# Turning the normed FFN rows in the cross-attention stage, with their combinations stored turned

## The chip, the cores and the metric

One NeuronCore of a Trainium2 chip runs the whole kernel. Its engines are TensorE (PE, with its weight loads listed apart as PEld), VectorE (DVE), ScalarE (ACT), GpSimd (POOL) and the queue engine SyncE (SP), which issues most DMAs; POOL issues the others. Matrix products come out in PSUM, 16 KB in each of 128 partitions; everything else is in SBUF or, between stages, in DRAM. The metric is the device time of one execution in microseconds, the median of several runs.

## What is computed

One layer of a streaming encoder for 2048 prompt rows and 128 sample rows of width 1024: a mixer (banded attention beside a convolution), a cross attention into 256 memory rows, and a SwiGLU FFN, each with a norm ahead of it and one behind. The part that matters here:

```python
h = rmsnorm(x, g_mem_pre)
x = x + rmsnorm(memory_attention(h, mk, mv, w_mq, w_mo), g_mem_post)
h = rmsnorm(x, g_ffn_pre)
f = (jax.nn.silu(h @ w_gate) * (h @ w_up)) @ w_down      # 1024 -> 2816 -> 1024
x = x + rmsnorm(f, g_ffn_post)
```

All in float32. The kernel makes each product from three: both operands are split into a rounded high part and a low part, and hi*hi, hi*lo and lo*hi are summed in PSUM (`mm3`, lines 286 to 290, or `mm3h`, lines 292 to 297).

## The kernel before, in words

**Order of the work.** A tile scheduler sets the order on each engine: it takes the instructions in program order as priority, simulates the engines' times, and adds the semaphores that the data need. Each engine then runs its list in order. Buffers are fixed places in SBUF and PSUM: a `Region` gives each tag a list of places, and one request after the other takes the next place in the list (`at`, `tile`). Two tags may share a place; a later user then waits until the earlier one, in program order, is through.

**Cross attention** (`phase_cross`). Sixteen prompt tiles of 128 rows. The pass of the loop for tile t holds, in program order: `probs` of t (8 transposes of the probabilities into PSUM "t", then a cast on ACT, L1317, and a subtract on DVE, L1318), `scores` of t+1 (48 matmuls of 512 columns, L296, into "s"), `norm` of t+2 (a normed tile, 8 transposes into "t"), `values` of t (48 matmuls into "y", then `postnorm`, L341 to L347: square on ACT (L313), rstd on POOL, scale on DVE (L345), residual add on POOL (L346), store of the tile to `x2` in DRAM). "t" is one buffer at 8 KB of PSUM, "s" one at 12 KB, "y" two at 4 and 0 KB. For tiles 14 and 15 the order is a little different: `probs` of 15 stands in the midst of the values of 14.

**`natural`** (L1331 to L1354). The FFN goes over three groups of rows, `GROUPS`, of up to 384 columns each. It multiplies with fewer products by combining halves, so it wants, for each pair of row tiles (`PAIRS`, three for each group, the last of group 2 being the two halves of the sample tile, 64 rows each), seven combinations of the halves of the two normed tiles, 512 columns wide. `natural` loads the two tiles of a pair into `na` and `nb`, norms them (square L1342, rstd on POOL L1344 and L1345, scale on DVE L1346), makes combinations with four POOL adds (L1347, 1349, 1351, 1353) in `na`, `nb` and `nt`, and stores them with four POOL DMAs to `hn` in DRAM. `na`, `nb` and `nt` are single, at SBUF 0 to 12 KB. The square writes the single scratch buffer `junk`, as the square of `postnorm` does. One pair is done at the end of a pass of the loop as soon as its tiles are there: after t = 4, 5, 6 (group 0), 7 (the sample pair), 10, 11, 12 (group 1) and 15 (pair (2,0)). Pair (2,1) is left for gate-up.

**Gate-up** (`gate_up`). For each group g and each of 22 blocks f of 128 hidden columns: 7 products of 12 matmuls each (`product`, L288 to L290) between a weight combination (`wforms`, made on POOL from two 512 KB loads and split by L1446 on ACT and L1447 on DVE) and a row combination `ts[j]`. The row combinations of a group are made by `tform` (L1415 to L1428): for each of seven, three loads of 256 KB from `hn` (buffer "nat": three of 2 KB), 4 transposes each into PSUM "tr" (L1424), a cast on ACT (L1426) and a subtract on DVE from PSUM (L1427). For group 0 this stands at the start, with raised priority; for groups 1 and 2 between the products of the last block of the group before (`turn`), each combination right behind the product that used its place last: these are the two turns. The products write PSUM places of 2 KB in the order 8, 10, 0, 2, 4, 6 KB.

Of the kernel before, what the change touches and what calls it, by code (L numbers as in the profile page):

```python
# [8 lines left out]
F32 = mybir.dt.float32  # L9
# [3 lines left out]
ALU = mybir.AluOpType  # L13
# [4 lines left out]
P = 128  # L18
D = 1024
KC = D // P  # L20
# [31 lines left out]
TFORM = (0, 5, 1, 2, 4, 6, 3)  # L52
# [34 lines left out]
class Region:  # L87
# [13 lines left out]
    def at(self, tag, kb, *places):  # L101
        self.tags[tag] = [[arena.find(int(o * 256)) for arena, offs in places for o in offs], int(kb * 256), 0]
        return self
# [35 lines left out]
class Build:  # L139
# [82 lines left out]
    def setup(self):  # L222
        nc, A = self.nc, self.A
        enter = lambda n, **kw: self.ctx.enter_context(self.tc.tile_pool(name=self.nm(n), bufs=1, **kw))
        self.const = enter("const")
        self.dpool = enter("dram", space=DRAM)
        sb, ps = enter("sb"), enter("ps", space=PSUM)
        self.sbF = Arena(sb.tile([P, 13120], F32, tag="f", name="sbf"))
        sbr = Arena(sb.tile([P, 22528], F32R, tag="r", name="sbr"))
        self.xctx = ExitStack()  # L230
        sx = self.xctx.enter_context(self.tc.tile_pool(name=self.nm("sx"), bufs=1))
        self.sbR = Joined(sbr, Arena(sx.tile([P, 5120], F32R, tag="x", name="sbx")))
        self.ps = Arena(ps.tile([P, 4096], F32, tag="p", name="psb"))
        self.ident = self.t(self.const, [P, P], F32, "ident")
        make_identity(nc, self.ident)
        self.mhalf = self.t(self.const, [P, 4], F32, "mhalf")
        nc.gpsimd.memset(self.mhalf[:, :], -0.5)
        self.f1s = self.dram("f1s", [P, KC, MH, NM])
        self.f2s = self.dram("f2s", [P, KC, D])
        self.qs = [self.dram(f"qs{i}", [P, 2, NPT * P]) for i in range(4)]  # L240
        self.ks = [self.dram(f"ks{i}", [2, P, NPT * P]) for i in range(4)]
        self.vs = [self.dram(f"vs{i}", [P, 4, NPT, P]) for i in range(2)]
        self.cs = [self.dram(f"cs{i}", [P, 4 * P]) for i in range(NPT + 1)]
        self.x1 = [self.dram(f"x1_{i}", [P, D]) for i in range(NPT + 1)]
        self.x2 = [self.dram(f"x2_{i}", [P, D]) for i in range(NPT + 1)]
        self.hn = [self.dram(f"hn{g}", [P, 3, 7, 512]) for g in range(3)]
        self.af = [self.dram(f"af{g}", [P, NF // 2, 7, 3 * P]) for g in range(3)]
        self.vsamp = self.dram("vsampd", [P, 512])

# [1007 lines left out]
    def phase_cross(self, ctx):  # L1257
        nc, A = self.nc, self.A
        sbF, sbR = self.sbF, self.sbR
# [68 lines left out]

        gffn = self.gain(Region().at("gffn", 4, (self.gffn, [0])), "g_ffn_pre", "gffn")

        def natural(g, p):  # L1331
            n = PAIRS[g][p][2]
            xa = self.t(pool, [P, 2, 512], F32, "na")[:n]
            xb = self.t(pool, [P, 2, 512], F32, "nb")[:n]
            tt = self.t(pool, [P, 2, 512], F32, "nt")[:n]
            dst = self.hn[g]
            for x, (t, r0) in zip((xa, xb), PAIRS[g][p][:2]):
                x2 = x.rearrange("p a b -> p (a b)")
                nc.sync.dma_start(x2, self.x2[t][r0:r0 + n, :])
                junk = self.t(pool, [P, D], BF16, "junk", 1)  # L1340
                ss = self.t(pool, [P, 1], F32, "ss", 6)
                nc.scalar.activation(junk[:n, :], x2, AF.Square, accum_out=ss[:n, :])  # L1342
                r = self.t(pool, [P, 1], F32, "rstd", 6)
                nc.gpsimd.tensor_scalar(r[:n, :], ss[:n, :], 1.0 / D, EPS, ALU.mult, ALU.add)  # L1344
                nc.gpsimd.tensor_tensor(r[:n, :], r[:n, :], self.mhalf[:n, 0:1], ALU.pow)  # L1345
                nc.vector.scalar_tensor_tensor(x2, x2, r[:n, :], gffn[:n, :], ALU.mult, ALU.mult)  # L1346
            nc.gpsimd.tensor_tensor(tt[:, 0, :], xb[:, 0, :], xa[:, 0, :], ALU.subtract)  # L1347
            nc.gpsimd.dma_start(dst[:n, p, 0:2, :], xa)
            nc.gpsimd.tensor_tensor(tt[:, 1, :], xb[:, 1, :], tt[:, 0, :], ALU.subtract)
            nc.gpsimd.dma_start(dst[:n, p, 4:6, :], tt)  # L1350
            nc.gpsimd.tensor_tensor(xb[:, 0, :], xb[:, 1, :], xb[:, 0, :], ALU.subtract)
            nc.gpsimd.dma_start(dst[:n, p, 2:4, :], xb)
            nc.gpsimd.tensor_tensor(xa[:, 1, :], tt[:, 1, :], xa[:, 1, :], ALU.subtract)
            nc.gpsimd.dma_start(dst[:n, p, 6, :], xa[:, 1, :])  # L1354

        self.natural = natural
        todo = [(g, p) for g in range(3) for p in range(3)]
        hq = {0: norm(0)}
        f1 = [load(self.f1s[:, k, :, :].rearrange("p h n -> p (h n)"), f"f1{k}",
# [11 lines left out]
        for t in range(NPT):  # L1371
            pp = probs(z) if t < NPT - 1 else self.last_probs
            if t == 0:
                more(KC, self.last_split)
            if t + 1 < NPT:
                z = scores(*hq[t + 1][1:])
            if t + 2 < NPT:
                hq[t + 2] = norm(t + 2)
            values(t, hq.pop(t)[0], *pp)
            for g, p in list(todo):  # L1380
                ready = all(x == S_TILE or x < t for x, _ in PAIRS[g][p][:2])
                if ready and t >= 4:
                    natural(g, p)
                    todo.remove((g, p))
                    break
        self.todo = todo
# [9 lines left out]
    def gate_up(self, ctx):  # L1396


        nc, A = self.nc, self.A
        sbF, sbR = self.sbF, self.sbR  # L1400
        t6h, t6l, w8, fx, af0, af1 = self.flex(ctx, (1536, F32R), (1536, F32R), (1024, F32R), (1536, F32), (2688, F32),
                                               (2688, F32))
        pool = (Region().at("wf", 4, (sbF, [12, 18, 46.5, 22]))
                .at("s", 2, (sbF, [26, 28, 38.5])).at("nat", 2, (sbF, [40.5, 42.5, 44.5]))
                .at("x1", 1.5, (sbF, [30, 31.5])).at("x2", 1.5, (sbF, [33, 34.5]))
                .at("x3", 1.5, (sbF, [36]), (fx, [0])).at("th", 1.5, (fx, [1.5, 3, 4.5]))
                .at("wh", 2, (sbR, [68, 72, 76, 80, 84, 88, 92, 104]), (w8, [0]))
# [7 lines left out]
        def tform(g, j):  # L1415
            hi = self.t(pool, [P, 4, 3 * P], F32R, f"t{j}h")
            lo = self.t(pool, [P, 4, 3 * P], F32R, f"t{j}l")
            for p in range(3):
                n = PAIRS[g][p][2]
                x = self.t(pool, [P, 512], F32, "nat")  # L1420
                nc.sync.dma_start(x[:n, :], self.hn[g][:n, p, TFORM[j], :])
                ps = self.t(ps_tr, [P, 4, P], F32, "tr")
                for k in range(4):
                    nc.tensor.transpose(ps[:, k, :n], x[:n, k * P:(k + 1) * P], self.ident[:n, :n])  # L1424
                c = slice(p * P, p * P + n)
                nc.scalar.copy(hi[:, :, c], ps[:, :, :n])  # L1426
                nc.vector.tensor_tensor(lo[:, :, c], ps[:, :, :n], hi[:, :, c].bitcast(F32), ALU.subtract)  # L1427
            return hi, lo  # L1428

        def wforms(f):  # L1430
# [30 lines left out]
        for g in range(3):  # L1461
            n = sum(p[2] for p in PAIRS[g])
            for fp in range(NF // 2):
# [4 lines left out]
                for x in range(2):  # L1468
# [45 lines left out]
                    if f < NF - 1 or g < 2:  # L1514
                        w = wforms((f + 1) % NF)
                    if g == 0 and x == 1 and self.todo:
                        self.natural(*self.todo.pop(0))
                self.act_forms(af, g)
                nc.sync.dma_start(self.af[g][:, fp, :, :], af[:, :, :])

# [208 lines left out]
```

## Time and profile before

| what | value |
|---|---|
| median of 3 runs | 3008.1 us (3006.9 to 3008.7) |
| span of the profiled execution | 3000.1 us; the page gives no time of that execution apart from its span |
| PE busy | 2949.2 us |
| cross attention, first to last square of a finished tile (L313) | 1232.5 to 1577.0 us |
| gate-up, first matmul of 384 columns to the end of its stage | 1576.8 to about 2517 us |
| transposes in `tform` (L1424) | 252, at 1564.0 to 2284.1 us |
| turns to group 1 and group 2 | near 1885 to 1960 and 2225 to 2300 us |

The profile is one execution, on one core. Rows of the timeline give start and length in us, engine, line, operation, output and input by the program's names, the number of instructions merged, and in brackets the idle time of the engine ahead of them with what ended it. Matmuls are pipelined: a row's length is longer than the step from one matmul to the next. A row of the windows view gives a stretch and the time that each engine was busy in it; PEclk is the granted TensorE clock as a share of full speed.

### The profile page before, as it was taken

How to read it: one execution, taken by the hardware profiler on the slowest of the kernel's cores; microseconds unless marked ns; L12 is line 12 of the kernel's file. 1: busy time of each engine (PE TensorE's matmuls, PEld its weight loads, DVE VectorE, ACT ScalarE, POOL GpSimd, SP SyncE). 2: the span in 40 equal slices, each digit the busy share in tenths (PEclk: the TensorE clock that was granted, in tenths of full speed). 3: DMA queues.
4: the chain of work that ended last, by engine and by line, in shares of the span. 5: the costliest groups of instructions: out<-in, count | busy, mean ns of one | idle time of the engine just before them, and what ended most of it. 6: DMA issues, size and time to landing. Idle time of an engine off the chain costs nothing.

```text
span 3000.1 us, 46145 instructions
## 1 busy us (share of the span) xinstructions
PE 2949.2 (98%) x16940; PEld 2714.6 (90%) x16940; DVE 2134.6 (71%) x3090; ACT 1360.3 (45%) x2731; POOL 1416.7 (47%) x1338
## 2 busy tenths in 40 slices
PE   9999999999999999999999999999999999999998
PEld 9999999989997887887888999999999999888777
DVE  6687886968776466435358888888788998555666
ACT  5535455668883344323334333433344444433433
POOL 0267496721123244136357565446555775424413
PEclk9999999989999999999999999999999999999999
DMA  7645253664435456323246333544334336756664
GB/s 278 246 138 185 88 170 108 201 213 168 155 138 175 169 199 205 105 87 133 88 163 222 116 137 124 196 153 152 134 134 157 142 140 205 256 176 215 217 223 148
DMA packets 197552, 499.57 MB, mean 167 GB/s; under 512 B 19334, under 2 KB 84750, under 8 KB 188485
## 3 DMA queue, kind: packets, MB, share of 16 engines
q1 hardware_dynamic: 182397, 427.01, 41.9%
q0 software_dynamic: 14928, 69.61, 6.2%
q8 instruction: 133, 2.18, 0.3%
q14 instruction: 94, 0.77, 0.1%
HBM read 365.45 MB, written 141.81 MB: 169 GB/s over the span
## 4 chain that ended last, share of the span: by engine, by line
PE 38%; DMA 4%; issue 3%; DVE 3%; POOL 3%; ACT 0%; SPq 0%; DVEq 0%; POOLq 0%; ACTq 0%
PE psb L290 12%; PE psb L288 12%; PE psb L289 12%; DMA sbf<-in_w_down_dram 2%; POOL sbf L1569 1%; PE psb L296 1%; DMA sbf<-x 1%; PE psb L1424 1%; DMA sbf<-hn 0%; DVE sbr L1639 0%; DVE sbr L1447 0%; POOL sbf L346 0%; DVE sbr L1573 0%; DMA sbf<-in_w_gate_dram 0%; DVE sbx L1447 0%
## 5 line engine op out<-in xcount | busy, mean ns | idle before, releaser
L288 PE MATMUL psb<-sbr 128*128 128x384 f32 (+3 forms) x2808 | 941.7, 337 | 4.1 <-DVE sbx L676 1.6
L289 PE MATMUL psb<-sbr 128*128 128x384 f32 (+3 forms) x2356 | 804.6, 342 | 0.4 <-DVE sbr L338 0.3
L290 PE MATMUL psb<-sbr 128*128 128x512 f32 (+3 forms) x1848 | 633.1, 344 | 4.3 <-DVE sbr L1639 4.1
L288 PEld LDWEIGHTS psb<-sbr 128*128 128x128 f32 x2808 | 529.2, 189 | 34.6 <-ACT sbr L1638 2.8
L290 PE MATMUL psb<-sbr,sbx 128*128 128x384 f32 (+2 forms) x1484 | 475.8, 321 | 0.0
L289 PEld LDWEIGHTS psb<-sbr 128*128 128x128 f32 x2356 | 443.9, 188 | 27.1 <-DVE sbr L1427 0.7
L290 PEld LDWEIGHTS psb<-sbr 128*128 128x128 f32 x1848 | 347.9, 188 | 34.9 <-DVE sbr L1639 8.2
L296 PE MATMUL psb<-sbr 128*128 128x512 f32 x1200 | 295.3, 394 | 1.9 <-ACT sbr L1317 1.1
L1447 DVE TENSOR_TENSOR sbr<-sbf,sbr 128x512 fp32r<-128x512 f32 x258 | 262.7, 1021 | 38.8 <-ACT sbr L1446 37.9
L1446 ACT CAST sbr<-sbf 128x512 fp32r<-128x512 f32 x258 | 159.2, 620 | 277.4 <-PE psb L289 229.3
L290 PEld LDWEIGHTS psb<-sbr,sbx 128*128 128x128 f32 x1484 | 279.6, 189 | 0.2
L542 DVE SCALAR_TENSOR_TENSOR psb<-sbf,psb 128x768 f32<-128x768 f32 (+1 forms) x290 | 264.3, 911 | 6.1
L296 PEld LDWEIGHTS psb<-sbr 128*128 128x128 f32 x1200 | 222.2, 189 | 47.6 <-ACT sbr L1317 1.3
L1639 DVE TENSOR_TENSOR sbr<-sbf,sbr 128x384 fp32r<-128x384 f32 (+2 forms) x242 | 168.1, 717 | 99.2 <-ACT sbr L1638 98.0
L283 POOL TENSOR_TENSOR sbx<-sbf,sbr 128x1024 fp32r<-128x1024 f32 (+1 forms) x62 | 155.0, 2501 | 84.8 <-ACT sbr L281 81.0
L1638 ACT CAST sbr<-sbf 128x384 fp32r<-128x384 f32 (+2 forms) x242 | 112.4, 483 | 174.1 <-PE psb L289 149.8
L1569 POOL TENSOR_TENSOR sbf<-sbf 128x512 f32<-128x512 f32 x77 | 106.5, 1390 | 168.7 <-DMA sbf<-in_w_down_dram 167.1
L552 POOL TENSOR_TENSOR flexb<-flexb,flexb 128x128 f32<-128x128 f32 (+1 forms) x180 | 168.9, 939 | 25.4 <-ACT flexb L551 15.1
L288 PE MATMUL psb<-sbr,sbx 128*128 128x384 f32 (+1 forms) x524 | 170.6, 327 | 1.8 <-ACT sbx L1446 1.1
L1446 ACT CAST sbx<-sbf 128x512 fp32r<-128x512 f32 x153 | 94.7, 620 | 163.4 <-PE psb L289 143.4
L1447 DVE TENSOR_TENSOR sbx<-sbf,sbx 128x512 fp32r<-128x512 f32 x153 | 153.4, 1004 | 17.0 <-ACT sbx L1446 16.8
L1441 POOL TENSOR_TENSOR sbf<-sbf 128x512 f32<-128x512 f32 x66 | 97.5, 1477 | 107.2 <-DVE sbr L1447 50.7
(350 smaller groups left out, 6281.5 us busy)
## 6 DMA issues: line engine op xcount, KB each, us to landing
af<-flexb SPq DMA_DIRECT2D x33, 1344.0 KB, 5.8
sbf<-in_w_down_dram SPq DMA_DIRECT2D x154, 256.0 KB, 3.5
sbf<-in_w_gate_dram SPq DMA_DIRECT2D x66, 512.0 KB, 3.3
sbf<-in_w_up_dram SPq DMA_DIRECT2D x66, 512.0 KB, 3.5
sbf<-af SPq DMA_DIRECT2D x85, 384.0 KB, 4.3
sbf<-x SPq DMA_DIRECT2D x49, 512.0 KB, 3.8
sbf<-in_w_in_dram SPq DMA_DIRECT2D x48, 512.0 KB, 3.8
sbr<-ks POOLq DMA_DIRECT2D x16, 1024.0 KB, 8.6
```

What stands on the lines that cost most here:

```text
L283: self.lo_engine.tensor_tensor(lo[:, c], wf[:, c], hi[:, c].bitcast(F32), ALU.subtract)
L288: nc.tensor.matmul(ps, lh, rh, start=start, stop=False, **kw)
L289: nc.tensor.matmul(ps, lh, rl, start=False, stop=False, **kw)
L290: nc.tensor.matmul(ps, ll, rh, start=False, stop=stop, **kw)
L296: nc.tensor.matmul(y[o], l, r[:, o * 512:(o + 1) * 512], start=start and x == 0, stop=stop and x == 2)
L542: nc.vector.scalar_tensor_tensor(acc if w < CW - 1 else o, src(w), cwt[:, j, w:w + 1], acc, ALU.mult, ALU.add)
L552: nc.gpsimd.tensor_tensor(o, o, v, ALU.add)
L1446: nc.scalar.copy(hs[j][:, :], src[j])
L1447: nc.vector.tensor_tensor(ls[j][:, :], src[j], hs[j][:, :].bitcast(F32), ALU.subtract)
L1569: nc.gpsimd.tensor_tensor(acc[:, :], acc[:, :], q[:, :], ALU.add if s > 0 else ALU.subtract)
L1638: nc.scalar.copy(ch[:, m], a[:, x, m])
L1639: nc.vector.tensor_tensor(cl[:, m], a[:, x, m], ch[:, m].bitcast(F32), ALU.subtract)
```

## The change

`natural` becomes `forms`. It still loads and norms the two tiles of a pair, and then turns each of them: 8 transposes into a PSUM buffer that the caller names ("t" in the cross attention, one buffer for all 8; "tr" in gate-up, two of 4), and two copies on ACT back into the tile's own place, so that `na` and `nb` hold their normed rows turned. The four POOL adds work on the turned tiles as before on the unturned ones, and the four stores write `hn`, which is laid out as 128 partitions by 7 combinations by the three pairs' columns.

`tform` loads a combination of the whole group with one DMA of up to 768 KB, and splits it straight from SBUF: one cast and one subtract for 1536 columns (for group 2 two of each, since its last pair is narrower). Its transposes are gone. "nat" is three buffers of 6 KB in place of three of 2 KB: the first where the three were, at 40.5 KB, the others at 0 and 6 KB of SBUF, on the places of `na`, `nb` and `nt`.

```diff
--- before.py
+++ after.py
@@ -243,7 +243,7 @@
         self.cs = [self.dram(f"cs{i}", [P, 4 * P]) for i in range(NPT + 1)]
         self.x1 = [self.dram(f"x1_{i}", [P, D]) for i in range(NPT + 1)]
         self.x2 = [self.dram(f"x2_{i}", [P, D]) for i in range(NPT + 1)]
-        self.hn = [self.dram(f"hn{g}", [P, 3, 7, 512]) for g in range(3)]
+        self.hn = [self.dram(f"hn{g}", [P, 7, 3 * 512]) for g in range(3)]
         self.af = [self.dram(f"af{g}", [P, NF // 2, 7, 3 * P]) for g in range(3)]
         self.vsamp = self.dram("vsampd", [P, 512])
 
@@ -1328,14 +1328,11 @@
 
         gffn = self.gain(Region().at("gffn", 4, (self.gffn, [0])), "g_ffn_pre", "gffn")
 
-        def natural(g, p):
+        def forms(g, p, pspool, tag, step):
             n = PAIRS[g][p][2]
-            xa = self.t(pool, [P, 2, 512], F32, "na")[:n]
-            xb = self.t(pool, [P, 2, 512], F32, "nb")[:n]
-            tt = self.t(pool, [P, 2, 512], F32, "nt")[:n]
-            dst = self.hn[g]
+            xa, xb, tt = [self.t(pool, [P, 2, 512], F32, f"n{c}") for c in "abt"]
             for x, (t, r0) in zip((xa, xb), PAIRS[g][p][:2]):
-                x2 = x.rearrange("p a b -> p (a b)")
+                x2 = x[:n].rearrange("p a b -> p (a b)")
                 nc.sync.dma_start(x2, self.x2[t][r0:r0 + n, :])
                 junk = self.t(pool, [P, D], BF16, "junk", 1)
                 ss = self.t(pool, [P, 1], F32, "ss", 6)
@@ -1344,16 +1341,29 @@
                 nc.gpsimd.tensor_scalar(r[:n, :], ss[:n, :], 1.0 / D, EPS, ALU.mult, ALU.add)
                 nc.gpsimd.tensor_tensor(r[:n, :], r[:n, :], self.mhalf[:n, 0:1], ALU.pow)
                 nc.vector.scalar_tensor_tensor(x2, x2, r[:n, :], gffn[:n, :], ALU.mult, ALU.mult)
+                parts = []
+                for k0 in range(0, KC, step):
+                    ps = self.t(pspool, [P, step, P], F32, tag)
+                    for k in range(step):
+                        nc.tensor.transpose(ps[:, k, :n], x2[:, (k0 + k) * P:(k0 + k + 1) * P], self.ident[:n, :n])
+                    parts.append(ps)
+                for k0, ps in zip(range(0, KC, step), parts):
+                    for a in range(k0 // 4, (k0 + step) // 4):
+                        nc.scalar.copy(x[:, a, :4 * n].rearrange("p (k q) -> p k q", q=n),
+                                       ps[:, 4 * a - k0:4 * a - k0 + 4, :n])
+            w = 4 * n
+            xa, xb, tt = (x[:, :, :w] for x in (xa, xb, tt))
+            at = lambda j, m: self.hn[g][:, j:j + m, p * 512:p * 512 + w]
             nc.gpsimd.tensor_tensor(tt[:, 0, :], xb[:, 0, :], xa[:, 0, :], ALU.subtract)
-            nc.gpsimd.dma_start(dst[:n, p, 0:2, :], xa)
+            nc.gpsimd.dma_start(at(0, 2), xa)
             nc.gpsimd.tensor_tensor(tt[:, 1, :], xb[:, 1, :], tt[:, 0, :], ALU.subtract)
-            nc.gpsimd.dma_start(dst[:n, p, 4:6, :], tt)
+            nc.gpsimd.dma_start(at(4, 2), tt)
             nc.gpsimd.tensor_tensor(xb[:, 0, :], xb[:, 1, :], xb[:, 0, :], ALU.subtract)
-            nc.gpsimd.dma_start(dst[:n, p, 2:4, :], xb)
+            nc.gpsimd.dma_start(at(2, 2), xb)
             nc.gpsimd.tensor_tensor(xa[:, 1, :], tt[:, 1, :], xa[:, 1, :], ALU.subtract)
-            nc.gpsimd.dma_start(dst[:n, p, 6, :], xa[:, 1, :])
-
-        self.natural = natural
+            nc.gpsimd.dma_start(at(6, 1), xa[:, 1:2, :])
+
+        self.forms = forms
         todo = [(g, p) for g in range(3) for p in range(3)]
         hq = {0: norm(0)}
         f1 = [load(self.f1s[:, k, :, :].rearrange("p h n -> p (h n)"), f"f1{k}",
@@ -1380,7 +1390,7 @@
             for g, p in list(todo):
                 ready = all(x == S_TILE or x < t for x, _ in PAIRS[g][p][:2])
                 if ready and t >= 4:
-                    natural(g, p)
+                    forms(g, p, ps_t, "t", KC)
                     todo.remove((g, p))
                     break
         self.todo = todo
@@ -1401,7 +1411,7 @@
         t6h, t6l, w8, fx, af0, af1 = self.flex(ctx, (1536, F32R), (1536, F32R), (1024, F32R), (1536, F32), (2688, F32),
                                                (2688, F32))
         pool = (Region().at("wf", 4, (sbF, [12, 18, 46.5, 22]))
-                .at("s", 2, (sbF, [26, 28, 38.5])).at("nat", 2, (sbF, [40.5, 42.5, 44.5]))
+                .at("s", 2, (sbF, [26, 28, 38.5])).at("nat", 6, (sbF, [40.5, 0, 6]))
                 .at("x1", 1.5, (sbF, [30, 31.5])).at("x2", 1.5, (sbF, [33, 34.5]))
                 .at("x3", 1.5, (sbF, [36]), (fx, [0])).at("th", 1.5, (fx, [1.5, 3, 4.5]))
                 .at("wh", 2, (sbR, [68, 72, 76, 80, 84, 88, 92, 104]), (w8, [0]))
@@ -1415,16 +1425,15 @@
         def tform(g, j):
             hi = self.t(pool, [P, 4, 3 * P], F32R, f"t{j}h")
             lo = self.t(pool, [P, 4, 3 * P], F32R, f"t{j}l")
-            for p in range(3):
+            x = self.t(pool, [P, 3 * 512], F32, "nat")
+            w = 512 * 2 + 4 * PAIRS[g][2][2]
+            nc.sync.dma_start(x[:, :w], self.hn[g][:, TFORM[j], :w])
+            for p, m in ((0, 3),) if g < 2 else ((0, 2), (2, 1)):
                 n = PAIRS[g][p][2]
-                x = self.t(pool, [P, 512], F32, "nat")
-                nc.sync.dma_start(x[:n, :], self.hn[g][:n, p, TFORM[j], :])
-                ps = self.t(ps_tr, [P, 4, P], F32, "tr")
-                for k in range(4):
-                    nc.tensor.transpose(ps[:, k, :n], x[:n, k * P:(k + 1) * P], self.ident[:n, :n])
-                c = slice(p * P, p * P + n)
-                nc.scalar.copy(hi[:, :, c], ps[:, :, :n])
-                nc.vector.tensor_tensor(lo[:, :, c], ps[:, :, :n], hi[:, :, c].bitcast(F32), ALU.subtract)
+                src = x[:, p * 512:p * 512 + m * 4 * n].rearrange("q (p k c) -> q p k c", p=m, k=4)
+                h, l = (y[:, :, p * P:p * P + m * n].rearrange("q k (p c) -> q p k c", p=m) for y in (hi, lo))
+                nc.scalar.copy(h, src)
+                nc.vector.tensor_tensor(l, src, h.bitcast(F32), ALU.subtract)
             return hi, lo
 
         def wforms(f):
@@ -1514,7 +1523,7 @@
                     if f < NF - 1 or g < 2:
                         w = wforms((f + 1) % NF)
                     if g == 0 and x == 1 and self.todo:
-                        self.natural(*self.todo.pop(0))
+                        self.forms(*self.todo.pop(0), ps_tr, "tr", 4)
                 self.act_forms(af, g)
                 nc.sync.dma_start(self.af[g][:, fp, :, :], af[:, :, :])
 
```

## The prediction

> **What bounds the kernel now.** I read the page's totals first, then a windows view cut at the stages that the edit touches, then the instructions in order of time.
>
> ```profile
> PE 2949.2 (98%) x16940; PEld 2714.6 (90%) x16940; DVE 2134.6 (71%) x3090; ACT 1360.3 (45%) x2731; POOL 1416.7 (47%) x1338
> ```
> ```profile
> 1298.99:1322.56 23.57, 23.57 (x114) 19.68 (x113) 7.38 (x10) 6.24 (x15) 4.51 (x6) 1.00 0.21 67
> 1322.56:1420.42 97.86, 94.89 (x450) 78.44 (x449) 52.81 (x48) 32.82 (x72) 60.05 (x72) 1.00 0.38 136
> 1467.56:1540.66 73.10, 71.11 (x338) 58.85 (x337) 39.09 (x36) 24.62 (x55) 45.13 (x54) 1.00 0.44 160
> 1576.75:1611.00 34.25, 28.03 (x162) 24.86 (x161) 25.75 (x31) 17.59 (x33) 26.68 (x24) 0.95 0.78 257
> 1885.00:1960.00 75.00, 72.08 (x443) 70.50 (x442) 58.16 (x87) 32.86 (x62) 32.27 (x24) 1.00 0.58 195
> 2225.00:2300.00 75.00, 74.92 (x494) 72.42 (x493) 62.09 (x98) 36.91 (x71) 40.02 (x33) 1.00 0.44 153
> ```
> The columns are stretch, length, busy time of PE, PEld, DVE, ACT and POOL, granted clock, DMA share and GB/s. TensorE is the bound. A plain tile of the cross attention takes 23.57 us, all of it PE (first row). The second and third rows are four and three tiles, each with a `natural` in it: 97.86 - 4 x 23.57 = 3.6 and 73.10 - 3 x 23.57 = 2.4, together 6.0 us of waits. The fourth row is the start of gate-up, with 6.2 us of PE idle; the last two are its turns to the next group.
>
> So removed transposes pay one for one, and added ones cost one for one, if nothing new waits. What may wait shows in the first tile with a `natural` (E, the end of its values, is at 1322.56):
>
> ```profile
> 1322.56 1.02 ACT L313 ACTIVATE sbf<-psb 128x1024 bf16<-128x1024 f32 x1 [5.44 <-PE psb L296]
> ...
> 1323.75 1.06 ACT L1342 ACTIVATE sbf<-sbf 128x1024 bf16<-128x1024 f32 x1
> ...
> 1325.85 1.28 DVE L1346 SCALAR_TENSOR_TENSOR sbf<-sbf,flexb 128x1024 f32<-128x1024 f32 x1
> 1325.98 3.41 POOL L346 TENSOR_TENSOR sbf<-sbf 128x1024 f32<-128x1024 f32 x1 [0.17 <-DVE sbf L345]
> ...
> 1331.51 1.28 DVE L1346 SCALAR_TENSOR_TENSOR sbf<-sbf,flexb 128x1024 f32<-128x1024 f32 x1 [3.24 <-POOL sbf L1345]
> ...
> 1334.05 1.52 PE L296 MATMUL psb<-sbr 128*128 128x512 f32 x6
> 1335.41 1.28 POOL L1347 TENSOR_TENSOR sbf<-sbf 128x512 f32<-128x512 f32 x1
> ...
> 1346.12 1.02 ACT L313 ACTIVATE sbf<-psb 128x1024 bf16<-128x1024 f32 x1 [4.33 <-PE psb L296]
> 1346.29 0.90 SPq L1339 DMA_DIRECT2D sbf<-x  x2
> ...
> 1358.62 1.28 DVE L1346 SCALAR_TENSOR_TENSOR sbf<-sbf,flexb 128x1024 f32<-128x1024 f32 x1 [0.93 <-POOL sbf L1345]
> ```
> The square of a pair's first tile (L1342) starts only behind the square of the values just finished (L313): both write the one buffer `junk`. The second tile's scaling (second L1346) ends at 1332.79, E + 10.2; it waited for its rstd on POOL, where the long residual add (L346) came first. In the next tile (E at 1346.12) it ends at 1359.90, E + 13.8. The next values begin at 1334.05, E + 11.5; until then PE has scores to do. All of this is hidden today.
>
> **The change, part by part.** *Transposes.* One price for both lines, and that of a matmul of 384 columns, from the chain of waits:
>
> ```profile
> 1919.28 0.87 PE psb L1424 x8
> 1920.16 0.17 PE psb L288
> ```
> Removed: 252, or 27.4 us. Added: 18 sets of 8 (9 pairs, 2 tiles each), 15.7 us. Net -11.7, were that all.
>
> *Cross attention, seven tiles (t = 4 to 7, 10 to 12).* Each gets 2 x 0.87 = 1.74 us of transposes: 12.2 us. But these write the PSUM buffer "t", of which there is one, and which `probs` of the next tile fills next in program order. The next probabilities now wait for the second scaling, its 8 transposes, two copies, then 8 transposes of their own, a cast (L1317) and a subtract (L1318):
>
> ```profile
> L1317 ACT CAST sbr<-psb x16: 994/1009/1020, 1214.8 to 1562.3; 128x1024 fp32r<-128x1024 f32 x16
> ```
> ```profile
> L1318 DVE TENSOR_TENSOR sbr<-psb,sbr x16: 1208/1214/1225, 1215.8 to 1563.4; 128x1024 fp32r<-128x1024 f32 x16
> ```
> ```profile
> L1426 ACT CAST sbr<-psb 128x512 fp32r<-128x512 f32 x18 | 10.4, 589 | 13.1 <-PE psb L1424 12.9
> L1446 ACT CAST sbr<-sbf 128x512 fp32r<-128x512 f32 x13 | 8.0, 619 | 7.8 <-PE psb L289 3.7 <-POOL sbf L1441 1.6 <-POOL sbf L1444 1.5
> ```
> ```profile
> L1447 DVE TENSOR_TENSOR sbr<-sbf,sbr 128x512 fp32r<-128x512 f32 x12 | 14.4, 1209 | 1.2 <-ACT sbr L1446 1.2
> L1427 DVE TENSOR_TENSOR sbr<-psb,sbr 128x512 fp32r<-128x512 f32 x15 | 10.0, 685 | 11.7 <-ACT sbr L1426 11.7
> ```
> 0.87 + 2 x 0.589 (L1426 does the like) + 0.87 + 1.01 + 1.21 = 5.1, and with some 0.1 for each handoff, an estimate from L346's 0.17, 5.6. The next values can start at E + 15.8. PE has work until E + 11.5 + 1.74 = E + 13.2 and then stands: behind the waiting `probs` come only the values that need it, the next norm's transposes (same buffer) and scores that need that norm. Stall 2.6 us a tile. Bounds: none if the scaling ends by E + 7.6; 6.2 us at E + 13.8. I take the first tile's, since the second's was late for its loads: the SPq row starts them at 1346.29, when the pair before had left its single buffers, 10.9 us after its first add (L1347). In a period stretched to 27.6 us those buffers are free at E + 12.3 (copies) + 10.9 = E + 23.2, ahead of the next E. The 6.0 us of waits (norms that come late) go, for norms get that much more time. Sum 12.2 + 7 x 2.6 - 6.0 = **+24**; bounds 12.2 - 6.0 = +6 and 12.2 + 7 x 6.2 = +56.
>
> *Start of gate-up.* Tile 15's pair (2,0) has the same chain, with no scores to hide it:
>
> ```profile
> 1577.01 1.02 ACT L313 ACTIVATE sbf<-psb 128x1024 bf16<-128x1024 f32 x1 [2.45 <-PE psb L296]
> ...
> 1587.23 1.27 DVE L1346 SCALAR_TENSOR_TENSOR sbf<-sbf,flexb 128x1024 f32<-128x1024 f32 x1
> ```
> ```profile
> 1576.75:1611.00 34.25, 9.11 (x60) 7.00 (x60) 0.95 0.78 257
> ```
> ```profile
> af<-flexb SPq DMA_DIRECT2D x33, 1344.0 KB, 5.8
> sbf<-in_w_down_dram SPq DMA_DIRECT2D x154, 256.0 KB, 3.5
> ```
> The second scaling ends at E + 11.5. The first product of gate-up writes PSUM from 8 KB on, which is that same "t": it now starts behind transposes and copies, at E + 13.7 (today at E). Then "nat": its second and third buffers now lie on `na`, `nb`, `nt` (SBUF 0 to 12 KB), free when the pair's last store has read them, 10.9 us later: E + 24.6. A 768 KB load I put at 4.6 us (between the rows for 256 and 1344 KB), its cast and subtract at three 512s each, 3 x (0.619 + 0.685) = 3.9: combination 1 is ready at E + 33. Until then PE has two products of combination 0 (12 matmuls of 0.174 each, 4.2 us). Today PE works 28.03 of the 34.25 us; 60 transposes (L1424's own row) take 6.5, so 21.5 are matmuls, against 4.2 + 1.0 after. Lost 16.3; this group's other 24 transposes come back (2.6), and the clock falls once more (1.7, below): **+15**. Bounds: +2 (scaling at E + 7.6, and combinations 3 and 6 loaded past the blocked ones through the first buffer) and +25 (each product waiting for its own load and split).
>
> *The two turns.* 168 transposes are 18.3 us, and of the 3.0 us of PE idle there about 2 are waits for loads that are now one of three. Against it, the subtract now reads SBUF twice. L1427 (one operand in PSUM) took 685 ns, L1447 (both in SBUF, POOL adding beside it) 1209: a turn's 21 units go from 14.4 to at most 25.4 us. DVE has 16.8 and 12.9 us idle at the two turns, less some 9 that PE gives back, so at most 3 and 7 us stick out; I take 4 in all. **-16**; bounds -21 and -8.
>
> The Trainium skill, "SBUF — State Buffer", section "SBUF: two separate sides", has a rule against this part: a DVE instruction with two SBUF inputs and a GpSimd instruction that reads SBUF exclude each other for a whole instruction. The two rows agree (685 against 1209). By the rule each of a turn's seven subtracts would wait for one POOL add of 1.28 us, 9 us; by the rows it is up to 11.
>
> *Pair (2,1)*, now transposed inside gate-up: 16 transposes, 1.7, and a short wait: **+2**, bounds 1.7 and 5. The stores keep their number and bytes; POOL issues them later by the copies and transposes, hidden behind scores except at tile 15, where it is counted.
>
> Sum: 24 + 15 - 16 + 2 = +25 on the span of 3000.1. The page gives no time of its own execution beside the span; the median 3008.1 lies 8.0 above it, and I carry that over: **3033 us**.
>
> **The rivals.** *The turning fits (faster).* If the second scaling is done by E + 7.6, PE never waits: cross +6, start +3, turns -21, pair +2: -10, 2998. For it: nothing in the data makes the residual add stand ahead of the second rstd. Against: in both tiles shown, and at tile 15, the scaling ends at E + 10 or later.
>
> *Stalls as in the second tile, and a falling clock (much slower).*
>
> ```profile
> 1590.00:1592.00 2.00, 0.19 (x2) 0.22 (x3) 1.56 (x2) 0.69 (x2) 1.92 (x2) 1.00 0.71 265
> 1592.00:1594.00 2.00, 1.96 (x10) 1.14 (x9) 0.90 (x2) 1.17 (x2) 2.00 (x3) 0.63 0.27 59
> 1594.00:1596.00 2.00, 2.00 (x7) 2.00 (x8) 0.48 (x1) 0.00 (x0) 1.98 (x3) 0.51 1.01 332
> ```
> After a stretch almost without PE the granted clock fell to 0.63 and 0.51: 0.37 x 2 + 0.49 x 2 = 1.7 us lost. With stalls of 6.2 us each of the seven tiles would pay it too: cross 7 x (1.74 + 6.2 + 1.7) = +67, start +20, turns -12, pair +2: +77, 3085. The Trainium skill, "TensorE: Matmul & The Clock Gate", section "The HAM clock gate (the "warmup" mystery)", puts the idle window at about 3.4 us; by that the stalls of my sum stay free of it. The trace agrees so far: the 6.0 us of waits in those tiles left the clock at 1.00.
>
> *The stalls are half as long (no change).* Cross +12, start +6, turns -18, pair +2: +2, 3010.
>
> **How the numbers follow.** Forecast (3018 to 3048) 0.48; much slower 0.16; no change 0.13; faster 0.23. A measurement of this kernel tells about 0.2%, 6 us, from no change: faster 0.23, same 0.13, slower 0.64. The range takes in most of both outer cases: 2996 to 3066.
>
> **What would show it.** Right: seven tiles near 27.6 us instead of 24.4; PE waiting ahead of the transposes of `probs` or of the values; the first gate-up matmul some 12 us behind the last values; loads of `hn` behind POOL's last store; turns 8 us shorter each. Wrong: tiles at 25.3 (23.57 + 1.74), or gate-up starting at E.

## The result, and the profile after

The kernel after takes 3077.3 us (median of 4 runs, 3072.6 to 3081.4), the kernel before 3007.5 us beside it (4 runs, 3006.8 to 3008.7): a ratio of 1.0241, 95% interval 1.0220 to 1.0263. It is slower, by 69.8 us where 25 were forecast, and outside the range. The span of the profiled execution went from 3000.1 to 3076.9 us. That is 76.8 us, 7 more than the medians differ by: where both are on record the span lies 1.8 us below the time, so the profile of before is of an execution of some 3002 us, quicker than its median. (Of the 8.0 us that the prediction carried over from span to median, most was that.)

The totals of the page of the kernel after:

```profile
PE 2969.4 (97%) x16832; PEld 2726.5 (89%) x16832; DVE 2145.2 (70%) x3055; ACT 1374.3 (45%) x2732; POOL 1419.2 (46%) x1338
```

PE has 108 instructions less and is yet busy 20 us longer: some of what is left runs slower. The windows view of the kernel after, cut as that of before: a plain tile, the four and the three tiles with a pair, the start of gate-up, and the two turns (each moved by as much as the stage had moved until there). Columns: stretch, length, busy PE, PEld, DVE, ACT, POOL, granted clock, DMA share, GB/s.

```profile
1302.19:1325.75 23.56, 23.56 (x114) 19.68 (x113) 7.38 (x10) 6.23 (x14) 4.50 (x6) 1.00 0.22 67
1325.75:1461.20 135.45, 114.45 (x515) 92.14 (x514) 48.01 (x48) 40.94 (x89) 56.89 (x72) 0.89 0.29 102
1508.35:1613.27 104.92, 87.54 (x387) 69.91 (x386) 35.40 (x36) 31.34 (x66) 44.28 (x54) 0.89 0.34 118
1650.20:1684.45 34.25, 16.56 (x56) 14.49 (x57) 15.36 (x11) 13.10 (x20) 21.32 (x20) 0.61 0.67 230
1971.30:2046.30 75.00, 71.36 (x403) 71.05 (x402) 71.38 (x85) 35.58 (x56) 39.44 (x27) 0.98 0.58 202
2303.20:2378.20 75.00, 69.81 (x435) 69.06 (x434) 73.12 (x95) 35.98 (x65) 42.92 (x34) 0.98 0.50 170
```

The plain tile is as it was, 23.56 us. The seven tiles with a pair take 135.45 + 104.92 = 240.37 us in place of 97.86 + 73.10 = 170.96: **69.4 us more**, 34.3 a tile where 27.6 were forecast, and at a granted clock of 0.89. So nearly the whole loss is there. The rest, by the times at which the stores of `af` in gate-up are issued, counted from the end of the last values: the first store comes 14.9 us later than before, and gate-up settles at +13.1; turn 1 brings that to +5.0, turn 2 to +1.8. Over the span: +3.2 ahead of the cross attention (its PE list is the same, so scatter), +70.0 in it, +1.5 in gate-up, +2.1 behind.

The timeline of the first tile with a pair, kernel after, shows where those 10 us of a tile go (E is 1325.75; start, length, engine, line, operation, count, and in brackets the idle time ahead and what ended it):

```profile
1334.17 1.28 DVE L1343 SCALAR_TENSOR_TENSOR sbf<-sbf,flexb 128x1024 f32<-128x1024 f32 x1 [3.85 <-POOL sbf L1342]
...
1336.46 1.06 ACT L313 ACTIVATE sbf<-sbf 128x1024 bf16<-128x1024 f32 x1 [7.13 <-DMA sbf<-x]
...
1337.51 1.05 ACT L1352 COPY sbf<-psb 128x512 f32<-128x512 f32 x2
...
1338.13 1.14 PE L1348 MATMUL psb<-ident,sbf 128*128 128x128 f32 x8 [0.71 <-ACT sbf L1352]
...
1339.46 1.14 PE L1314 MATMUL psb<-ident,sbf 128*128 128x128 f32 x8 [0.19 <-ACT sbf L1352]
...
1341.00 0.47 ACT L1303 ACTIVATE sbf<-psb,sbf 128x256 f32<-128x256 f32 x1 [1.10 <-DVE sbf L1299]
...
1342.37 0.48 ACT L1303 ACTIVATE sbf<-psb,sbf 128x256 f32<-128x256 f32 x1
...
1342.81 1.02 ACT L1317 CAST sbr<-psb 128x1024 fp32r<-128x1024 f32 x1
...
1343.18 3.09 DVE L1308 TENSOR_SCALAR sbf<-sbf 128x256 f32<-128x256 f32 x4
...
1343.89 2.07 PE L296 MATMUL psb<-sbr 128*128 128x512 f32 x4 [3.28 <-ACT sbr L1317]
...
1346.19 1.21 DVE L1318 TENSOR_TENSOR sbr<-psb,sbr 128x1024 fp32r<-128x1024 f32 x1
1347.45 1.97 PE L323 MATMUL psb<-ident,sbf 128*128 128x128 f32 x8 [1.49 <-DVE sbr L1318]
...
1350.07 3.22 PE L296 MATMUL psb<-sbx,sbr 128*128 128x512 f32 x8
```

The second tile's scaling (L1343) ends at 1335.45, E + 9.7, about where it did before. Its transposes (L1348) begin only at 1338.13: "t" holds the first tile's until the copies (L1352) have run, and these stand on ACT behind the next norm's square (L313), which waits for a load. The transposes of `probs` (L1314) are through at 1340.60, and then their cast (L1317) waits until 1342.81, though its data are there: four exponentials of the following tile (L1303) stand ahead of it in ACT's list. The subtract (L1318) could start at 1343.83 and starts at 1346.19: four normalisings of that tile (L1308, 3.09 us) stand ahead of it in DVE's list. PE stands for 3.28 and 1.49 us, and what comes between and behind runs at half the clock: 8 matmuls in 3.22 us.

The windows view in steps of 2 us over the same place shows the clock by itself (third number from the end):

```profile
1339.00:1341.00 2.00, 1.42 (x11) 0.87 (x9) 1.97 (x2) 0.90 (x2) 1.94 (x2) 1.00 0.41 156
1341.00:1343.00 2.00, 0.00 (x0) 0.00 (x0) 0.03 (x1) 2.00 (x9) 1.95 (x2) 0.86 0.28 107
1343.00:1345.00 2.00, 1.11 (x3) 0.92 (x4) 1.96 (x3) 0.83 (x1) 1.98 (x3) 0.50 0.12 47
...
1351.00:1353.00 2.00, 2.00 (x7) 1.56 (x6) 0.73 (x1) 0.00 (x0) 0.00 (x0) 0.58 0.87 313
1353.00:1355.00 2.00, 2.00 (x11) 1.61 (x10) 0.00 (x0) 0.00 (x0) 0.00 (x0) 1.00 0.06 25
```

In finer steps the clock is 0.50 from 1342.4 to 1352.7 us. And the start of gate-up, from the kernel after's timeline (E is 1650.20):

```profile
1660.16 1.28 DVE L1343 SCALAR_TENSOR_TENSOR sbf<-sbf,flexb 128x1024 f32<-128x1024 f32 x1 [0.46 <-POOL sbf L1342]
...
1661.59 1.94 PE L1348 MATMUL psb<-ident,sbf 128*128 128x128 f32 x8 [4.28 <-DVE sbf L1343]
...
1663.35 0.69 PE L288 MATMUL psb<-sbr 128*128 128x384 f32 x1
...
1673.19 0.57 POOL L1364 DMA_DIRECT2D hn<-sbf  x1
...
1677.19 1.47 ACT L1435 CAST sbr<-sbf 128x1536 fp32r<-128x1536 f32 x1 [1.95 <-DMA sbf<-hn]
```

The first product of gate-up stands behind the turn of pair (2,0) and begins at E + 13.2 (forecast E + 13.7). The next combination is cast (L1435) at E + 27.0, 4.0 us behind the pair's last store on POOL (L1364).

### The profile page after: what moved, and what is told of

The parts are those of the page before. It is cut to its first block, busy times and chain, and to the rows that moved or that the text cites. A ratio compares the mean times of both kernels' runs of the same rounds, so it can differ in the third digit from the quotient of the medians.

```text
span 3076.9 us, 45814 instructions
## 1 busy us (share of the span) xinstructions
PE 2969.4 (97%) x16832; PEld 2726.5 (89%) x16832; DVE 2145.2 (70%) x3055; ACT 1374.3 (45%) x2732; POOL 1419.2 (46%) x1338
## 4 chain that ended last, share of the span: by engine, by line
PE 38%; DVE 4%; DMA 3%; POOL 2%; issue 2%; ACT 1%; DVEq 0%; SPq 0%; POOLq 0%; ACTq 0%
PE psb L290 12%; PE psb L288 12%; PE psb L289 12%; DMA sbf<-in_w_down_dram 1%; PE psb L296 1%; POOL sbf L1578 1%; DVE sbr L1456 1%; DVE sbr L1648 1%; DVE sbr L1436 1%; DMA sbf<-x 1%; DMA sbf<-hn 1%; DVE sbx L1456 0%; DVE flexb L1511 0%; POOL sbf L346 0%; DVE sbf L363 0%
## 5 line engine op out<-in xcount | busy, mean ns | idle before, releaser
L296 PE MATMUL psb<-sbr 128*128 128x512 f32 x1200 | 305.9, 404 | 23.8 <-ACT sbr L1317 22.8
L296 PEld LDWEIGHTS psb<-sbr 128*128 128x128 f32 x1200 | 225.7, 193 | 70.8 <-ACT sbr L1317 24.7
L1456 DVE TENSOR_TENSOR sbr<-sbf,sbr 128x512 fp32r<-128x512 f32 x258 | 266.1, 1033 | 31.1 <-ACT sbr L1455 30.4
L1455 ACT CAST sbr<-sbf 128x512 fp32r<-128x512 f32 x258 | 159.4, 620 | 275.8 <-PE psb L289 240.8
L1456 DVE TENSOR_TENSOR sbx<-sbf,sbx 128x512 fp32r<-128x512 f32 x153 | 160.2, 1049 | 24.9 <-ACT sbx L1455 24.6
L1455 ACT CAST sbx<-sbf 128x512 fp32r<-128x512 f32 x153 | 94.8, 620 | 164.0 <-PE psb L289 155.9
```

The lines of the kernel that those rows point to most:

```text
L296: nc.tensor.matmul(y[o], l, r[:, o * 512:(o + 1) * 512], start=start and x == 0, stop=stop and x == 2)
L1455: nc.scalar.copy(hs[j][:, :], src[j])
L1456: nc.vector.tensor_tensor(ls[j][:, :], src[j], hs[j][:, :].bitcast(F32), ALU.subtract)
```

## The experiments

**Theory A**: the loss in the cross attention is one of order. The pair's turn goes through the single buffer "t" ahead of the next `probs`, so the next values wait, and what stands ahead of their split in the lists of ACT and DVE makes it worse. **Theory B**: it is the work itself (transposes, copies, and the POOL adds at the side of DVE), wherever it stands. Times are compared with runs of the kernel before on the same chip (3003.6 us for the first four, 3002.6 for the next four, 3001.8 for the last two).

**e1_y: the turn through "y", of which there are two.**

```diff
-                    forms(g, p, ps_t, "t", KC)
+                    forms(g, p, ps_y, "y", KC)
```

> The turned tiles go into the PSUM places of the values ("y", two of them, taken in turn) in place of the one buffer "t"; all work is kept. Theory A (the cost is the order through "t": the next probabilities wait for the pair's turning, and their split then comes late behind the norm's square, the exponentials and the normalising): the seven tiles with a pair fall from 31.4 to 35.9 us to about 25.5 (23.57 and 16 transposes), some -62 us, and the first product of gate-up no longer waits for "t": 3005 to 3018 us. Theory B (the cost is the added work itself, on engines that are full in those tiles): tiles stay above 31 us, 3060 or more.

Measured: 3016.7 us, ratio 1.0049 (1.0032 to 1.0066). The windows of e1_y, four and three tiles:

```profile
1326.06:1427.04 100.98, 100.89 (x515) 84.82 (x514) 46.32 (x48) 40.50 (x88) 54.78 (x72) 1.00 0.39 137
1474.18:1550.14 75.96, 75.96 (x387) 64.14 (x386) 35.52 (x36) 30.98 (x67) 43.27 (x54) 1.00 0.43 152
```

With the same number of instructions the seven tiles take 176.94 us, 25.3 each, which is 23.56 and two sets of transposes at 0.87; PE is idle for 0.1 us in all. The work costs 6.0 us over the seven, and 63.4 of the 69.4 are a matter of order. Theory B falls.

The other half of the expectation, the start of gate-up, brought nothing. Its first product no longer waits for "t": its matmuls run from 1584.33 us, ahead of the end of the last values (1587.59). But the second product comes only at 1606.98, when the split of its weights on ACT (L1455) is through, and gate-up settles at +16.7 against before, later than in the kernel after (+13.1):

```profile
1606.98 0.69 PE L288 MATMUL psb<-sbr,sbx 128*128 128x384 f32 x1 [6.33 <-ACT sbx L1455]
```

**e2_behind: the same "t", but each pair's turn in program order behind the next `probs`.**

```diff
+        def turn(t):
+            for g, p in list(todo):
+                ...
         for t in range(NPT):
+            if t < NPT - 1:
+                turn(t - 1)
...
-            for g, p in list(todo):
-                ...
+            if t == NPT - 1:
+                turn(t)
```

> Same work and same buffer "t", but in the program the pair's turning stands behind the next tile's probabilities. Theory A: the probabilities are free again, tiles 25 to 28 us (the turning now shares "t" with the next norm only), 3015 to 3035 us. Theory B: above 3060.

Measured: 3014.8 us, ratio 1.0043 (1.0023 to 1.0063). In the profiled run (3026.0 us) the tiles lie between 24.4 and 27.2 us, and the cross attention takes 358.3 us, against 344.5 before, 414.5 after and 351.6 in e1_y. The buffer can stay as it is if the critical user is first in line. Tiles above 25.3 have some waits left, which e1_y hasn't: now the next norm's transposes stand behind the pair's.

**e3_late: pair (2,0) is left for gate-up, where pair (2,1) is turned already.**

```diff
-                if ready and t >= 4:
+                if ready and 4 <= t < NPT - 1:
```

> Pair (2,0) is left for gate-up, as pair (2,1) is; the rest is the changed kernel. If the start of gate-up loses its 13 us to that pair (first product behind "t", loads of combinations behind its stores), they go but for the 2 us of its transposes: 3062 to 3068 us. If it loses them to three large loads in place of 21 small ones, nothing changes: 3073 to 3081.

Measured: 3055.8 us, ratio 1.0181 (1.0155 to 1.0206). The cross attention is as slow as after (416.8 us), but gate-up settles at -2.0 us against before, in place of +13.1, and ends at -17.9. So the late start of gate-up was pair (2,0), and not the large loads, which e3_late keeps. The time is below the 3062 to 3068 us that were expected: the turns too bring more here, 9.2 and 6.7 us in place of 8.1 and 3.2.

**e4_junk: the squares of a pair get their own scratch, so that they don't wait for the square of the values.**

```diff
-                junk = self.t(pool, [P, D], BF16, "junk", 1)
+                junk = self.t(pool, [P, D], BF16, "nt")
```

> The pair's squares write their scratch into the pair's own third buffer and no longer wait for the square of the finished values; "t" is kept. Theory A, with the chain starting at the end of the values: the second scaling ends some 6 to 10 us earlier, the probabilities come early enough, tiles near 26 us, 3020 to 3035 us. If the place of the transposes in TensorE's own list is what holds them, tiles stay above 31 us, 3060 or more.

Measured: 3029.3 us, ratio 1.0093 (1.0074 to 1.0113); tiles of 25.9 to 31.6 us, more than expected in five of seven. From e4_junk's timeline, the second of those tiles (E is 1341.53):

```profile
1344.42 1.09 PE L1348 MATMUL psb<-ident,sbf 128*128 128x128 f32 x8 [2.00 <-DVE sbr L325]
...
1349.92 1.03 PE L1348 MATMUL psb<-ident,sbf 128*128 128x128 f32 x8
...
1355.35 1.04 PE L1314 MATMUL psb<-ident,sbf 128*128 128x128 f32 x8
1356.42 1.02 ACT L1317 CAST sbr<-psb 128x1024 fp32r<-128x1024 f32 x1 [1.40 <-PE psb L1314]
...
1358.61 0.48 ACT L1303 ACTIVATE sbf<-psb,sbf 128x256 f32<-128x256 f32 x1 [1.16 <-DVE sbf L1299]
```

Both sets of transposes now stand among other PE work, and the cast of `probs` runs right behind its transposes, ahead of the exponentials. What is left are waits of another place (2.00 us for the split of a norm, L325). How early the pair is ready decides, as the first rival had it; an own scratch alone does most of it.

**e7_lists: the single "t" kept, and the exponentials and the normalising told to be issued behind the split of `probs`.**

```diff
-                self.last_exp = nc.scalar.activation(z[:, h, :], sv[:, h, :], AF.Exp, ...)
+                with ExitStack() as first:
+                    if self.last_split is not None:
+                        first.enter_context(self.tc.issue_after(self.last_cast.ins))
+                    self.last_exp = nc.scalar.activation(z[:, h, :], sv[:, h, :], AF.Exp, ...)
...
-            nc.vector.reciprocal(ri[:, :], sm[:, :])
+            with ExitStack() as first:
+                if self.last_split is not None:
+                    first.enter_context(self.tc.issue_after(self.last_split.ins))
+                nc.vector.reciprocal(ri[:, :], sm[:, :])
```

> The changed kernel with "t" kept, but the cast and the subtract of the next probabilities stand ahead of the exponentials and of the normalising in the lists of ACT and DVE. If the 7 us a tile by which my sum fell short are the split's place in those lists and the clock that falls in the longer wait, the seven tiles fall from about 34.3 to 28 to 30 us, 3033 to 3052 us. If they are something else (the place of the transposes, the stores), they stay above 32 us.

Measured: 3041.9 us, ratio 1.0129 (1.0110 to 1.0147). The windows of e7_lists:

```profile
1327.45:1441.57 114.12, 107.17 (x515) 86.77 (x514) 48.73 (x48) 41.13 (x89) 56.93 (x72) 0.97 0.35 121
1488.70:1574.55 85.85, 79.13 (x387) 63.59 (x386) 34.76 (x36) 31.41 (x67) 44.50 (x54) 1.00 0.41 144
```

And its timeline at the same place of the first tile (lines moved: cast L1323, exponentials L1306, subtract L1324):

```profile
1342.53 1.01 ACT L1323 CAST sbr<-psb 128x1024 fp32r<-128x1024 f32 x1 [0.75 <-PE psb L1320]
...
1343.44 0.48 ACT L1306 ACTIVATE sbf<-psb,sbf 128x256 f32<-128x256 f32 x1
1343.58 1.22 DVE L1324 TENSOR_TENSOR sbr<-psb,sbr 128x1024 fp32r<-128x1024 f32 x1 [0.72 <-ACT sbr L1323]
1343.60 1.21 PE L296 MATMUL psb<-sbr 128*128 128x512 f32 x4 [1.10 <-ACT sbr L1323]
```

The split now runs as soon as its data are there, PE stands 1.10 us instead of 3.28, and four matmuls take 1.21 us instead of 2.07. The seven tiles take 199.97 us. That parts the 69.4: work less vanished waits 6.0 (e1_y against before), the buffer itself 23.0 (e7_lists against e1_y), and **the split's place in the lists 40.4** (after against e7_lists). Of the 40.4, 15.7 are PE busy for longer with the same instructions (201.99 against 186.30, so the clock) and 24.7 are idle. How much of it is ACT's list and how much DVE's wasn't parted. The clock fell once in the seven tiles of e7_lists, in the fourth, and that is in the 23.0. The parting is of the cross attention alone: gate-up settles at +22.1 in e7_lists, and why it is later than in the kernel after stays open.

**e5_both: e1_y and e3_late together.**

> The turned tiles in "y" and pair (2,0) left for gate-up, together. If the two costs are separate they add: the tiles stay at 25.3 us (cross attention 7 us over the kernel before), the start of gate-up loses no more than 2 us and the turns keep their gain, so gate-up ends 12 to 18 us ahead: 0.2 to 0.4% faster than the kernel before. If the start was lost to the three large loads, or the turning in "y" needs the time that (2,0) gives back, it is no faster than it.

Measured: 2995.9 us (12 runs), ratio 0.9979 (0.9970 to 0.9988), 0.2% faster than before. Cross attention 353.2 us; gate-up -0.9 after its start, -10.5 after turn 1, -15.7 at its end. Both losses of order are out, and what is left is what the transposes bring.

**e6_thirds and e10_start: on e5_both, the split of a combination in three pieces of 512 columns**, for all groups and for group 0 alone.

```diff
-            for p, m in ((0, 3),) if g < 2 else ((0, 2), (2, 1)):
+            for p, m in ((0, 1), (1, 1), (2, 1)):
```

> As e5_both, with the split of a combination in three casts and three subtracts of 512 columns in place of one of 1536; the load stays one. If the turns lose time because a long subtract stands ahead of the evictions that free PSUM in DVE's list, they get shorter by 2 to 5 us each. If DVE is simply full there, nothing changes or the extra instructions cost up to 2 us a turn.

> As e5_both, with the split in three parts for group 0 alone, where the first products wait for it, and in one (two for group 2) at the turns. If both findings hold, the start keeps the 5 us that the thirds gained there and the turns keep their 15: 2989 to 2993 us, 0.3 to 0.5% faster than the kernel before. If the thirds' gain at the start was chance, as e5_both, 2996.

Measured: e6_thirds 2995.6 us, ratio 0.9975 (0.9966 to 0.9985); e10_start 2997.0 us, ratio 0.9981 (0.9970 to 0.9992). Neither differs from e5_both. Small pieces do start gate-up 5.5 us earlier (-6.5 and -6.2 instead of -0.9), but the gain doesn't last: in e6_thirds turn 1 brings 3.4 us in place of 9.4, and in e10_start turn 2 brings 1.7 in place of 5.2. Both expectations of a lasting gain missed: gate-up ends at -15.7 and -16.1, as in e5_both (-15.7). Why turn 2 of e10_start, whose code is that of e5_both there, gives so little stays open.

**e8_pool: on e5_both, every second subtract of groups 1 and 2 on GpSimd.**

```diff
-                nc.vector.tensor_tensor(l, src, h.bitcast(F32), ALU.subtract)
+                (nc.gpsimd if g > 0 and j % 2 else nc.vector).tensor_tensor(l, src, h.bitcast(F32), ALU.subtract)
```

> As e5_both, with the subtracts of combinations 1, 3 and 5 of groups 1 and 2 on POOL. If DVE bounds the turns, they get 3 to 6 us shorter each. If POOL's longer subtracts (about 3.8 us for 1536 columns, from 1.3 for 512) block DVE meanwhile, nothing is gained or up to 5 us a turn is lost.

Measured: 3003.4 us, ratio 1.0002 (0.9992 to 1.0011). Turn 1 brings 3.5 us in place of 9.4. There a subtract on GpSimd takes 3.5 to 4.0 us, and one of those left on DVE takes 5.0 us instead of 1.75, for which PE stands 3.7 us. GpSimd is no better place.

**e9_nolow: on e5_both, without the subtracts of groups 1 and 2.** Their low parts stay those of group 0, so the kernel leaves out part of the computation.

```diff
-                nc.vector.tensor_tensor(l, src, h.bitcast(F32), ALU.subtract)
+                if g == 0:
+                    nc.vector.tensor_tensor(l, src, h.bitcast(F32), ALU.subtract)
```

> As e5_both, and tform leaves out its subtracts for groups 1 and 2: their low parts stay those of group 0, so part of the computation is missing. If DVE bounds the turns, each gets 3 to 6 us shorter, 2984 to 2990 us. If what holds the turns is the loads or the casts, no more than 2 us in all, 2993 to 2997.

Measured: 2982.5 us, ratio 0.9930 (0.9904 to 0.9955). The windows at the two turns, first e5_both, then e9_nolow:

```profile
1890.80:1965.80 75.00, 71.76 (x410) 70.53 (x409) 70.08 (x84) 35.47 (x57) 39.30 (x27) 1.00 0.55 198
2221.20:2296.20 75.00, 69.40 (x426) 68.61 (x425) 73.62 (x93) 35.93 (x65) 46.39 (x36) 0.95 0.49 170
```

```profile
1892.00:1967.00 75.00, 75.00 (x435) 75.00 (x434) 57.59 (x83) 37.56 (x59) 44.51 (x31) 1.00 0.56 208
2219.00:2294.00 75.00, 75.00 (x490) 75.00 (x489) 66.37 (x90) 39.46 (x72) 53.94 (x42) 1.00 0.54 196
```

With the subtracts DVE is busy 70 to 74 of the 75 us and PE waits 3 to 6; without them PE waits for nothing, and the turns bring about 13.6 and 14.5 us in place of 9.4 and 5.2: 4.2 and 9.3 us, the second more than the 3 to 6 expected. What PE waits for at the turns of e5_both is hardly ever a low part, but an add on DVE that empties a PSUM place (L1506, 2.7 of 3.2 us and 5.4 of 5.6). DVE is the bound of the turns once PE's transposes are out.

## Why the prediction was wrong

- **Plain tiles, and the price of a transpose: right.** e1_y gives 6.0 us for the work of the seven tiles less the waits that vanish; 12.2 - 6.0 = 6.2 was the forecast. (The 27.6 us a tile that the prediction names is 27.9 by its own terms, 23.57 + 1.74 + 2.6.)
- **That the single buffer "t" makes the next values wait: right**, shown by e1_y and e2_behind. Its own price is 23.0 us (e7_lists against e1_y, the copies' place behind the norm's square and one fall of the clock in it), where 7 x 2.6 = 18.2 was the forecast. The scaling ended at E + 9.6 or 9.7 in all seven tiles, forecast E + 10.2.
- **The step that failed** is the sum from the scaling to the next values: "its 8 transposes, two copies, then 8 transposes of their own, a cast (L1317) and a subtract (L1318)", put at 5.6 us. It took 12.0 (1335.45 to 1347.45). It had each of these start when its data were there. But ACT and DVE run their lists in order: the second tile's transposes stood 2.7 us for the first tile's copies, 1.9 of them because the copies stood behind the next norm's square (1335.57 to 1337.51); the cast stood behind exponentials (2.2), the subtract behind the normalising (2.4). With the last two of these out of the way e7_lists takes 7.7. That is 40.4 us, with the fall of the clock, against a forecast of nothing. The row that would have told it was in the trace of before, in its timeline of the same tile (E is 1322.56):

```profile
1324.81 1.00 ACT L1317 CAST sbr<-psb 128x1024 fp32r<-128x1024 f32 x1
1327.05 1.22 DVE L1318 TENSOR_TENSOR sbr<-psb,sbr 128x1024 fp32r<-128x1024 f32 x1
...
1338.95 0.47 ACT L1303 ACTIVATE sbf<-psb,sbf 128x256 f32<-128x256 f32 x1 [4.42 <-DVE sbf L1299]
```

  The cast stood 14.1 us ahead of the exponentials. It was to move from E + 2.3 to some E + 13, near their E + 16.4; in the kernel after they come at E + 15.3 and it at E + 17.1.
- **The clock: put at nothing, and it fell in all seven tiles.** It was left to a rival, for stalls of 6.2 us. The Trainium skill, "TensorE: Matmul & The Clock Gate", section "The HAM clock gate (the "warmup" mystery)", has the clock halved after an idle window of about 3.4 us, and on that the sum stayed at full clock. In the trace no single idle stretch of the first tile is over 3.28 us, and the clock was halved all the same, 1.8 us into that stretch and 5.0 us after the last matmuls of 512 columns (1337.42), with 2.3 us of transposes between. The half-clock stretches of the seven tiles last 6.83 us five times and 10.24 us twice, which is two and three steps of 3.41 us, and they begin whole numbers of such steps apart (1342.43, 1379.98, 1414.11: 11 and 10 steps). So the trace can be cut into these steps. The step ahead of the first fall, and two steps in a row of the second tile, the second of them ahead of its fall (PE's busy time behind the length, clock third from the end):

```profile
1339.02:1342.43 3.41, 1.40 (x11) 0.85 (x9) 1.95 (x2) 2.31 (x9) 3.31 (x4) 1.00 0.40 154
1373.15:1376.57 3.42, 2.29 (x16) 1.67 (x16) 2.42 (x2) 2.06 (x5) 2.82 (x5) 1.00 0.25 95
1376.57:1379.98 3.41, 0.57 (x3) 0.49 (x4) 1.46 (x3) 2.79 (x9) 3.39 (x4) 1.00 0.16 59
```

  Ahead of the seven falls PE was idle for 1.55 to 3.28 us of the step; it need not be the whole step. The step from 1373.15, with 16 transposes and nothing else, kept the clock, so transposes do count as work (so did a step of e7_lists, from 1500.93, with just as many). In e7_lists the stretch without matmuls of 512 columns, with as many transposes, lasted 4.5 us (to 1343.60), and the four matmuls behind it ran at 0.30 us each, with the clock at 1.00: no step of its seven tiles has over 1.34 us of idle PE, and the clock fell in one of them, after 1.31 us. So the border lies near there in these traces; no run tried it apart.
- **Start of gate-up: right in size, its waits open.** Forecast +15, and +2 for pair (2,1); measured +13.1 for both; e3_late shows that it hangs on pair (2,0). But the first product behind "t", with which the forecast begins, doesn't decide: without that wait gate-up settles at +16.7 (e1_y). With the pair in its place the runs lie between +13.1 and +22.1 (e7_lists), so the nearness of the number is partly luck.
- **The turns: forecast -16, measured -11.3** (-8.1 and -3.2). That DVE gives part of it back was right, the mechanism wasn't. The dearer subtracts did not come: the seven at turn 1 took 14.2 us in all, as the 21 of before did (14.3 us: 15 x 0.682, 3 x 0.692 and 3 x 0.689). From the view of line L1436, kernel after:

```profile
L1436 DVE TENSOR_TENSOR sbr<-sbf,sbr x5: 1745/1745/2851, 1993.0 to 2009.9; 128x1536 fp32r<-128x1536 f32 x5
...
L1436 DVE TENSOR_TENSOR sbx<-sbf,sbr x1: 1746/1746/1746, 2013.7 to 2013.7; 128x1536 fp32r<-128x1536 f32 x1
L1436 DVE TENSOR_TENSOR flexb<-sbf,flexb x1: 2603/2603/2603, 2018.6 to 2018.6; 128x1536 fp32r<-128x1536 f32 x1
```

  Most take 1.745 us, that is 582 ns for 512 columns, and only two are longer; that POOL held these up isn't shown. The row that the subtracts were priced from (1209 ns) is one mean among several for such a subtract: 942, 782 and 1344 ns for the three groups of L1447 at turn 1 of the kernel before. DVE bounds the turns by its whole load (e9_nolow). What grew in the 75 us of turn 1 was other work, the weights' subtracts above all, from 29 in 27.1 us (L1447, before) to 34 in 34.3 us (L1456, after).
- **The rivals.** "Much slower" came nearest with 3085 us, and it had the falling clock, but not its reason: it needed the scaling at E + 13.8, which came in none of the seven tiles. "Fits" was not what happened, but its mechanism is real: e4_junk, which readies the pair earlier, takes 369.9 us for the cross attention and so gets 45 of the 70 us back.

## What to carry to other kernels

A single buffer is an order: a new user that stands ahead of a critical one in program order hands all its own waits on, so give it a buffer that is free anyway (e1_y) or put it behind (e2_behind). And an instruction that a new wait holds back doesn't start when the wait ends but when its engine's list comes to it: before pricing an added wait, look in the trace at what follows the held instruction on its engine, because the next schedule may put that ahead. Here two edits of order turn 70 us lost into 0.2% gained (e5_both), and the transposes saved were worth little more, because the engine next in line, DVE, had only 17 and 13 us of slack at the two turns.

## What the runs showed of the hardware

The clock fell without one long gap: with idle stretches of 0.71, 0.19 and 3.28 us around two sets of eight transposes (1.14 us a set) it went to 0.50, 1.8 us into the last of them, and stayed there for 10.24 us; four matmuls of 512 columns then took 2.07 us instead of 1.21. The falls of the seven tiles lie on steps of 3.41 us, each behind a step in which PE was idle for 1.55 us or more, while a step filled with 2.29 us of transposes alone kept the clock. Over the seven tiles PE was busy 15.7 us longer than in e7_lists with the same instructions, more than the transposes themselves take (12.2).
